# Row sums' accumulators and late results in PSUM, new load sizes and a burst of unread products in a cross-entropy kernel

## The chip, the cores and the metric

One core of a Trainium2 chip runs the program. ScalarE, VectorE and TensorE are its engines here; they run side by side and wait for one another, and for transfers (DMA), by counters called semaphores. SBUF and PSUM are its two on-chip memories. The metric is the device time of one execution in microseconds (us). A kernel's time is the median of its runs; most kernels here spread by 0.2 to 0.7 us from run to run, so a difference of a few tenths needs several runs of both kernels on the same chip. "Same" means within 2% with the whole of the 95% interval.

## The reference

For each of 256 rows of 32000 fp32 logits, the result is the negative logarithm of the softmax at the row's label.

```python
log_probs = logits - np.max(logits, axis=-1, keepdims=True)
log_probs = log_probs - np.log(np.sum(np.exp(log_probs), axis=-1, keepdims=True))
return np.array([-log_probs[i, labels[i]] for i in range(batch)])
```

The kernel computes it as log(sum of exp(x)) minus the label's logit, without the maximum, as log(sum × exp(-x_label)). The logits are drawn from a normal distribution, so no exp overflows.

## The kernel before

Two rows lie behind one another on each of 128 partitions: 64000 columns in 14 loads, counted from 0. ScalarE takes each load's exp in place, and its accumulator gives the sum of that load. Every exp is therefore two instructions on the engine: the exp itself and a read that puts the accumulator into a column of `parts`. Load 3 holds the end of row 0 and the start of row 1 and takes two exps. One VectorE reduction per row adds its columns, one TensorE product per row multiplies the sum with exp(-x_label) (on a diagonal) and brings all partitions into one lane, and ScalarE takes the logarithm of that. The last load's sum skips the reduction and is added by a second product for row 1.

```python
CHUNKS = [
    1024, 14528, 13376, 8960, 7168, 5056, 3584,
    2816, 2176, 1536, 1280, 1024, 768, 704,
]
# ...
parts = [small.tile([P, n_of[r]], F32, name=f"parts{r}") for r in range(ROWS)]   # SBUF
s_last = small.tile([P, 1], F32, name="s_last")
lane = [psum.tile([1, P], F32, name=f"lane{r}") for r in range(ROWS)]
# ...
def exps(i):
    t, base = tiles[i]
    for a, b, r in pieces[i]:
        if i == last:
            acc = s_last[:, :]
        else:
            acc = parts[r][:, seen[r]:seen[r] + 1]
            seen[r] += 1
        nc.scalar.activation(
            out=t[:, a - base:b - base], in_=t[:, a - base:b - base],
            func=AF.Exp, accum_out=acc,
        )
# ... the end:
for i in range(done, last):
    exps(i)
    if i == turn:                      # the load in which row 0 ends
        nc.vector.reduce_sum(out=sums[:, 0:1], in_=parts[0][:, :], axis=mybir.AxisListType.X)
        nc.tensor.matmul(lane[0][:, :], sums[:, 0:1], diag[0][:, :], start=True, stop=True)
    if i == turn + 1:
        log_row(0)
nc.vector.reduce_sum(out=sums[:, 1:2], in_=parts[1][:, :], axis=mybir.AxisListType.X)
nc.tensor.matmul(lane[1][:, :], sums[:, 1:2], diag[1][:, :], start=True, stop=False)
exps(last)
nc.tensor.matmul(lane[1][:, :], s_last[:, :], diag[1][:, :], start=False, stop=True)
log_row(1)
# ... store
```

## Time and profile before

| | before |
|---|---|
| time, median of 3 (range) | 84.87 us (84.86 to 84.89) |
| span of the profile | 83.0 us |
| ScalarE busy | 58.2 us, 70% |
| DMA queue of the logits, share of 16 engines | 93.0% |
| last exp starts | 79.17 us |
| logarithm of row 1 starts | 80.71 us |

The prediction shows the lines on which it rests. Two more of the timeline of before are needed here, around the exp of load 4 (columns: start, length in us, engine, line, operation, result and source, shapes):

```profile
56.08 0.19 ACT L120 ACTIVATION_READ_ACCUMULATOR x<-x 128x1 f32 x1
56.17 6.16 ACT L120 ACTIVATE x<-x 128x7168 f32<-128x7168 f32 x1
```

The next exp starts 0.09 us after the accumulator read starts, while the read's record (0.19) is still open. This distance, read start to next exp start, is called the step below.

### The profile page before, as it was taken

Reading aid. Unit: us, or ns where it says so; the run is one execution under the profiler, and the core shown is the slowest. Engines: PE = TensorE matmul, PEld = TensorE weight load, DVE = VectorE, ACT = ScalarE, POOL = GpSimd, SP = SyncE. Lnnn points to the kernel's source line nnn. Section 1 sums busy time; section 2 is a strip of 40 time slices with the busy share of each in tenths; the row PEclk is TensorE's granted clock in tenths of the full one; section 3 lists DMA queues with packets and bytes.
Section 4 is the critical chain, followed back from the end, with each engine's and each line's share of the span. In section 5 each row is a group of like instructions: output and inputs, shape, how many; then the busy total and the mean of one; then the engine's idle time right before and its main releaser. Section 6 shows DMA issues by size and latency. Waiting matters only on the chain.

```text
span 83.0 us, 126 instructions
## 1 busy us (share of the span) xinstructions
PE 1.7 (2%) x6; PEld 0.3 (0%) x6; DVE 0.8 (1%) x4; ACT 58.2 (70%) x34; POOL 3.0 (4%) x10
## 2 busy tenths in 40 slices
PE   0000000000000000000000002000000000000050
PEld 0000000000000000000000000000000000000000
DVE  0000000000000000000000020000000000000000
ACT  6230000000899999029999999999999999999960
POOL 3000000000640000000000000000000000000000
DMA  4999999999999999979989799999999999999600
GB/s 87 614 448 448 448 448 448 448 448 413 412 412 413 412 413 412 412 328 501 449 380 535 307 401 428 442 451 390 458 411 414 431 434 408 400 415 405 262 0 0
DMA packets 2226, 32.77 MB, mean 395 GB/s; under 512 B 433, under 2 KB 434, under 8 KB 1202
## 3 DMA queue, kind: packets, MB, share of 16 engines
q1 hardware_dynamic: 2018, 32.77, 93.0%
q10 hardware_dynamic: 144, 0.00, 0.1%
q0 software_dynamic: 64, 0.00, 0.1%
HBM read 32.77 MB, written 0.00 MB: 395 GB/s over the span
## 4 chain that ended last, share of the span: by engine, by line
DMA 43%; ACT 37%; issue 14%; PE 1%; SPq 0%; DVE 0%
DMA x<-in_logits_dram 43%; ACT x L120 26%; ACT x_tail L120 11%; PE lane L172 1%; PE lane L170 1%; ACT res L128 1%; SPq L108 0%; DVE sums L169 0%; ACT eg L159 0%
## 5 line engine op out<-in xcount | busy, mean ns | idle before, releaser
L120 ACT ACTIVATE x<-x 128x1024 f32<-128x1024 f32 (+7 forms) x8 | 46.3, 5786 | 21.3 <-DMA x<-in_logits_dram 21.3
L120 ACT ACTIVATE x_tail<-x_tail 128x2816 f32<-128x2816 f32 (+6 forms) x7 | 9.9, 1412 | 0.0
L144 POOL DMA_INDIRECT g<-in_logits_dram,idx x2 | 2.1, 1037 | 0.6 <-issue 0.3
L99 ACT ACT_TABLE_LOAD x1 | 1.3, 1283 | 0.8 <-PEq L191 0.8
L166 PE MATMUL lane<-diag,sums 128*1 128x128 f32 x2 | 0.6, 397 | 51.4 <-DVE sums L165 51.4
L120 ACT ACTIVATION_READ_ACCUMULATOR x<-x 128x1 f32 x8 | 1.5, 186 | 0.0
L120 ACT ACTIVATION_READ_ACCUMULATOR x_tail<-x_tail 128x1 f32 x7 | 1.3, 185 | 0.0
L170 PE MATMUL lane<-diag,sums 128*1 128x128 f32 x2 | 0.6, 397 | 27.5 <-DVE sums L169 27.5
L128 ACT ACTIVATE res<-lane 1x128 f32<-1x128 f32 x2 | 0.5, 266 | 0.7 <-PE lane L172 0.7
L161 DVE TENSOR_SCALAR diag<-ident,eg 128x128 f32<-128x128 f32 x2 | 0.5, 285 | 48.5 <-ACT eg L159 48.5
L142 POOL TENSOR_TENSOR idx<-idx,lbl 128x2 int32<-128x2 int32 x1 | 0.2, 193 | 19.6 <-DMA lbl<-in_labels_dram 19.6
L172 PE MATMUL lane<-diag,s_last 128*1 128x128 f32 x2 | 0.6, 398 | 0.0
L169 DVE TENSOR_REDUCE sums<-parts 128x1 f32<-128x10 f32 x1 | 0.2, 164 | 27.9 <-ACT x_tail L120 27.9
masks.py:199 POOL TENSOR_SCALAR_AFFINE_SELECT ident<-ident 128x128 f32<-128x128 f32 x1 | 0.3, 292 | 0.1
L166 PEld LDWEIGHTS lane<-diag,sums 128*1 128x1 f32 x2 | 0.1, 80 | 51.4 <-DVE sums L165 51.4
masks.py:197 POOL MEMSET ident<- 128x128 f32 x1 | 0.2, 194 | 0.0
L159 ACT ACTIVATE eg<-g 128x2 f32<-128x2 f32 x1 | 0.2, 187 | 0.0
L165 DVE TENSOR_REDUCE sums<-parts 128x1 f32<-128x4 f32 x1 | 0.2, 157 | 2.2 <-ACT x L120 2.2
L170 PEld LDWEIGHTS lane<-diag,sums 128*1 128x1 f32 x2 | 0.1, 80 | 28.0 <-DVE sums L169 28.0
L140 POOL IOTA idx<- 128x2 int32 x1 | 0.1, 120 | 0.5 <-POOLq L191 0.5
L191 POOL MEMSET const-uint8-127<- 128x1 uint8 x1 | 0.1, 118 | 0.0
L191 POOL MEMSET const-bfloat16-1.0<- 128x1 bf16 x1 | 0.1, 112 | 0.0
(3 smaller groups left out, 0.3 us busy)
## 6 DMA issues: line engine op xcount, KB each, us to landing
x<-in_logits_dram SPq DMA_DIRECT2D x1, 7264.0 KB, 20.1
x<-in_logits_dram SPq DMA_DIRECT2D x1, 6688.0 KB, 35.7
x<-in_logits_dram SPq DMA_DIRECT2D x1, 4480.0 KB, 45.8
x<-in_logits_dram SPq DMA_DIRECT2D x1, 3584.0 KB, 53.9
x<-in_logits_dram SPq DMA_DIRECT2D x1, 2528.0 KB, 59.3
x<-in_logits_dram SPq DMA_DIRECT2D x1, 1792.0 KB
x_tail<-in_logits_dram SPq DMA_DIRECT2D x1, 1408.0 KB, 21.0
x_tail<-in_logits_dram SPq DMA_DIRECT2D x1, 1088.0 KB, 23.1
```

The lines of the kernel that those rows point to most:

```text
L99: nc.scalar.preload_act_table_set("natural_log_exp_and_others")
L120: nc.scalar.activation(out=t[:, a - base:b - base], in_=t[:, a - base:b - base], func=AF.Exp, accum_out=acc,)
L128: nc.scalar.activation(out=res[0:1, r:ROWS * P:ROWS], in_=lane[r][:, :], func=AF.Ln)
L142: nc.gpsimd.tensor_add(out=idx[:, :], in0=idx[:, :], in1=lbl[:, 0:2 * ROWS:2])
L144: nc.gpsimd.indirect_dma_start(out=g[:, r:r + 1], out_offset=None, in_=logits[:, :], in_offset=bass.IndirectOffsetOnAxis(ap=idx[:, r:r + 1 ...
L159: nc.scalar.activation(out=eg[:, :], in_=g[:, :], func=AF.Exp, scale=-1.0)
L161: nc.vector.tensor_scalar_mul(diag[r][:, :], ident[:, :], eg[:, r:r + 1])
L165: nc.vector.reduce_sum(out=sums[:, 0:1], in_=parts[0][:, :], axis=mybir.AxisListType.X)
L166: nc.tensor.matmul(lane[0][:, :], sums[:, 0:1], diag[0][:, :], start=True, stop=True)
L169: nc.vector.reduce_sum(out=sums[:, 1:2], in_=parts[1][:, :], axis=mybir.AxisListType.X)
L170: nc.tensor.matmul(lane[1][:, :], sums[:, 1:2], diag[1][:, :], start=True, stop=False)
L172: nc.tensor.matmul(lane[1][:, :], s_last[:, :], diag[1][:, :], start=False, stop=True)
```

## The change

Its intent is to shorten the small costs of the end: accumulator reads and exp results go to PSUM, the load sizes are fitted to the cost per exp that this should give, and a burst of products whose results nobody reads keeps TensorE busy so that the last real product runs at its higher clock. The core of the diff:

```diff
 CHUNKS = [
-    1024, 14528, 13376, 8960, 7168, 5056, 3584,
-    2816, 2176, 1536, 1280, 1024, 768, 704,
+    1024, 15808, 12832, 9248, 6816, 4992, 3648,
+    2688, 2016, 1504, 1152, 928, 736, 608,
 ]
+WARM_FROM = 8
+WARM = 12
+TO_PSUM = 9
...
-    parts = [small.tile([P, n_of[r]], F32, name=f"parts{r}") for r in range(ROWS)]
+    acc_tile = psum.tile([P, sum(n_of)], F32, name="parts")
+    parts = [acc_tile[:, :n_of[0]], acc_tile[:, n_of[0]:]]
+    out_tile = psum.tile([P, max(CHUNKS[TO_PSUM:])], F32, name="x_out")
...
-    lane = [psum.tile([1, P], F32, name=f"lane{r}") for r in range(ROWS)]
+    lane_tile = psum.tile([1, ROWS * P], F32, name="lane")
+    lane = [lane_tile[:, r * P:(r + 1) * P] for r in range(ROWS)]
+    warm = psum.tile([1, P], F32, name="warm")
...
-                out=t[:, a - base:b - base],
+                out=t[:, a - base:b - base] if i < TO_PSUM else out_tile[:, :b - a],
...
+            if i == WARM_FROM:
+                at = starts[i] - tiles[i][1]
+                col = tiles[i][0][:, at:at + 1]
+                for _ in range(WARM):
+                    nc.tensor.matmul(warm[:, :], col, diag[0][:, :], start=True, stop=True)
```

More of the change, by code (lines that the diff above doesn't have):

```diff
@@ L128, in log_row @@
         nc.scalar.activation(
-            out=res[0:1, r:ROWS * P:ROWS], in_=lane[r][:, :], func=AF.Ln
+            out=res[0:1, r:ROWS * P:ROWS], in_=lane[r], func=AF.Ln
         )
@@ L164 @@
             if i == turn:
-                nc.vector.reduce_sum(out=sums[:, 0:1], in_=parts[0][:, :], axis=mybir.AxisListType.X)
-                nc.tensor.matmul(lane[0][:, :], sums[:, 0:1], diag[0][:, :], start=True, stop=True)
+                nc.vector.reduce_sum(out=sums[:, 0:1], in_=parts[0], axis=mybir.AxisListType.X)
+                nc.tensor.matmul(lane[0], sums[:, 0:1], diag[0][:, :], start=True, stop=True)
             if i == turn + 1:
                 log_row(0)
-        nc.vector.reduce_sum(out=sums[:, 1:2], in_=parts[1][:, :], axis=mybir.AxisListType.X)
-        nc.tensor.matmul(lane[1][:, :], sums[:, 1:2], diag[1][:, :], start=True, stop=False)
+            if i == WARM_FROM:
[3 more added lines that the diff above has]
+                    nc.tensor.matmul(warm[:, :], col, diag[0][:, :], start=True, stop=True)
+        nc.vector.reduce_sum(out=sums[:, 1:2], in_=parts[1], axis=mybir.AxisListType.X)
+        nc.tensor.matmul(lane[1], sums[:, 1:2], diag[1][:, :], start=True, stop=False)
         exps(last)
-        nc.tensor.matmul(lane[1][:, :], s_last[:, :], diag[1][:, :], start=False, stop=True)
+        nc.tensor.matmul(lane[1], s_last[:, :], diag[1][:, :], start=False, stop=True)
         log_row(1)
```

## The prediction

> **What bounds the kernel now.** I read the page's slices first, then the chain that ended last, then the timeline of the last 20 us, then the transfers. Two rows of the slices (40 slices of 2.08 us, busy tenths), ScalarE and the DMA engines:
>
> ```profile
> ACT  6230000000899999029999999999999999999960
> ...
> DMA  4999999999999999979989799999999999999600
> ```
>
> DMA is full from the first slice to 78 us. ScalarE waits for the first two large loads and is full from 37 us on. So two things run side by side for the last 40 us, and whichever is later at the last load sets the end. The chain gives the last steps (start, length in us):
>
> ```profile
> 66.80 3.36 ACT x L120 x3
> 70.15 9.12 ACT x_tail L120 x12
> 79.27 0.02 issue
> 79.30 0.17 DVE sums L169
> 79.47 0.04 issue
> 79.51 0.59 PE lane L170 x2
> 80.10 0.59 PE lane L172 x2
> 80.69 0.02 issue
> 80.71 0.27 ACT res L128
> ```
>
> The chain goes through ScalarE without a wait, then two 0.59 us TensorE products, the logarithm and the store. The timeline shows the steps of ScalarE:
>
> ```profile
> 62.04 0.33 SPq L108 DMA_DIRECT2D x_tail<-in_logits_dram  x1
> 62.24 0.19 ACT L120 ACTIVATION_READ_ACCUMULATOR x<-x 128x1 f32 x1
> 62.33 0.26 ACT L128 ACTIVATE res<-lane 1x128 f32<-1x128 f32 x1
> 62.49 4.40 ACT L120 ACTIVATE x<-x 128x5056 f32<-128x5056 f32 x1
> ...
> 72.50 0.18 ACT L120 ACTIVATION_READ_ACCUMULATOR x_tail<-x_tail 128x1 f32 x1
> 72.59 2.00 ACT L120 ACTIVATE x_tail<-x_tail 128x2176 f32<-128x2176 f32 x1
> 74.50 0.19 ACT L120 ACTIVATION_READ_ACCUMULATOR x_tail<-x_tail 128x1 f32 x1
> ...
> 79.17 0.77 ACT L120 ACTIVATE x_tail<-x_tail 128x704 f32<-128x704 f32 x1
> ```
>
> An exp of 2176 columns starts at 72.59, its accumulator read at 74.50: 1.91 us, which is 2176/1.2 = 1.813 plus 0.093. The next exp starts 0.093 after that read. So an exp costs its columns/1.2 plus 0.187 us, and each instruction starts 93 ns before the one ahead of it has ended. The last load is issued at 62.04:
>
> ```profile
> x_tail<-in_logits_dram SPq DMA_DIRECT2D x1, 352.0 KB, 16.9
> ```
>
> It lands at 62.04 + 16.9 = 78.95, and its exp starts at 79.17. **ScalarE is only 0.22 us behind DMA.** No reordering of ScalarE's work can gain more than that before the last exp; the rest must come after it.
>
> **What the skill says.** "Perfetto Trace Analysis", section Optimizing Scalar/DVE Operations: a ScalarE operation has about 93 ns of access on SBUF and 51 on PSUM, a VectorE one 60 and 125, and the profiled latency is about twice this because the acknowledgement overlaps with the next instruction. The trace agrees on SBUF: 93 ns and records of 186. It agrees on a PSUM source: the logarithm of 128 elements starts at 62.33 and the next exp 0.156 us later, 0.107 + 0.049. No run shows a PSUM destination yet. "ScalarE: Activation LUTs", section What ACT_TABLE_LOAD costs, gives 186 ns + 0.833 N and an overlap of 93, as the trace does. "PSUM — Partial Sum Buffer", section PSUM bank collisions raise a hardware error, says two engines may not touch one bank at once; that is why putting both rows' accumulators into one PSUM tile must bring waits. "TensorE: Matmul & The Clock Gate", section Part 1: The HAM clock gate, says the array runs at half clock until a free-running window of about 3.4 us has been busy, and falls back after an idle one. The trace has no clock record; its product takes 0.60 us from weights to semaphore, which I fit as two passes (the page counts two matmuls a product) of 0.213, 256 cycles at the page's 1.2 GHz, plus 0.17.
>
> **The change, part by part.**
>
> *Sizes.* From the transfer records a row of 58112 bytes takes 2.154 us on one engine and one of 2816 bytes 0.115, so a column costs 1.18 ns and a load about 0.09 us more. There are still 14 loads of the same total, so the last load lands at 78.95 as before. The loads before it move: load 2 (now 15808 + 12832 columns in) lands 736 columns, 0.87 us, later, at 37.74. Behind it ScalarE has 12832 and all later columns. With the old 0.187 per exp I step through, each start the later of landing and previous exp: load 3 at 48.73, load 4 at 56.81, 62.84, 67.19, 70.42, 72.84, 74.71, 76.15, 77.30, 78.26, and the last at 79.06. That is 0.11 before today's 79.17. The last exp is 96 columns shorter, another 0.08. Sum -0.19.
>
> *PSUM accumulators.* The built program of the changed kernel shows what the diff hides. In the kernel before, no exp behind another waits for it (one has a wait long satisfied). In the changed one **almost every exp waits on ScalarE's own semaphore**, for the accumulator read just before it, since they write one PSUM tile. So the 93 ns overlap is lost: the next exp starts not 93 ns after the read starts but after the read has ended, plus the semaphore. The semaphore shows 9 ns after a read's end, and a waiting engine starts about 22 ns later (VectorE at 79.296 after the update at 79.273). A read into PSUM I estimate at 2 x 51 = 102 ns from the skill's figures, so the step is 102 + 31 = 133 ns in place of 93: +0.04 per exp. It is paid by the second part of load 3 and by every load from 6 to 13: nine times, +0.36. Loads 3 and 5 hide it under the small exp and the logarithm.
>
> *The wait on VectorE.* The exp of load 4 now waits for the first row's sum, which itself waits for both parts of load 3. The path is: read 0.102, semaphore 0.032, reduction 0.16, semaphore and start 0.035, so 0.33 in place of 0.093: +0.24. ScalarE is on the path here and no slack takes it back, because all later landings are at its heels, not ahead.
>
> *Results in PSUM.* The next instruction starts after the source's access, which stays SBUF, so I give this nothing for the pace. The last accumulator stays in SBUF.
>
> *Unread products.* Twelve at 2 x 0.213 = 0.43 us make 5.1 us at the low clock. They start when the exp of load 8 is done, at about 75, and end about 79 to 80. If the clock rises, the last product takes 0.60 - 0.21 = 0.39 us: -0.21. The row-1 product is due about 0.24 us into the last exp, at 79.9, so the twelve are just out of the way.
>
> *Sum.* -0.11 - 0.08 - 0.21 + 0.36 + 0.24 = +0.20 us: 84.87 + 0.20 = **85.07**, say 85.0 with some weight on the rivals below.
>
> **Rivals.**
>
> *The new waits cost nothing* and a read into PSUM lets the next exp go after the skill's 51 ns. Then an exp costs about 0.15 (0.093 + 0.051) in place of 0.187, and ScalarE meets every landing within 0.1 us. For it: the new sizes fit exactly such an overhead; someone who saw exps fall behind would have put more columns in front. Against it: in this trace consumers of ScalarE's semaphore start only after the read's end. The last exp would start at 78.97: 79.17 to 78.97 is -0.20, with -0.08 and -0.21 about 84.4.
>
> *The waits cost more.* A read into PSUM may record 140 ns, between my 102 and the 186 that it has on SBUF: nine more of 0.038 and one on the VectorE path make +0.38, so about 85.4.
>
> *TensorE's clock does not rise, or the burst ends late.* Weight columns are one wide, and the window runs freely, so it may not count as busy in time. Without a rise +0.21; and with all twelve at the low clock from 75.2 they end at 80.3, after row 1's product is due, and would push it and the last product by up to 0.5. For it: 5.1 us is not much more than 3.4. About 85.3 to 85.6.
>
> *DMA becomes the bound.* It nearly is: nothing can start the last exp before 78.97. It caps the gain; it does not add.
>
> **Range and chances.** I give the costly self-waits about two chances in three, spread from 84.9 to 85.4 by the length of the read, and free ones one in three, near 84.4. The clock shifts either by 0.2. The middle of it all is 85.0; a range of 84.3 to 85.6 holds both. A change of 2% is 1.7 us. The gains stop at about 0.5 us since DMA bounds them, and the losses I can count stop near 1.0, so nearly all the chance is on within 2%.
>
> **What would show it.** In the changed profile: the start of the last exp (79.6 if the waits cost what I say, 79.0 if nothing); the time from an accumulator read's start to the next exp's (133 ns, against 93 before and about 51 for the rival) and the record of a read into PSUM (102); a gap of about 0.33 us ahead of the 6816-column exp; the last landing (78.95 unless the transfers change); the last product from its start to the logarithm's start (0.39 warm, 0.60 cold), and when the twelve end against row 1's product. The prediction is wrong in size if the read's record is not near 102, and wrong in kind if the read-to-exp step is shorter than 93 in spite of the waits, or if the late end comes from TensorE.

## More of the kernel before

The profile's span ends with the last instruction that it records. The profiled run took 84.82 us, so 1.79 us of its time lies outside its span (83.03 us in the trace).

## The result, and the profile after

| | before | after |
|---|---|---|
| time, median (range), 4 runs each | 84.88 us (84.86 to 84.90) | 86.37 us (86.19 to 86.52) |
| profiled run: time, span | 84.82, 83.0 us | 86.45, 84.3 us |
| exp of load 2 starts | 36.90 us | 38.28 us |
| last exp starts | 79.17 us | 80.73 us |
| logarithm of row 1 starts | 80.71 us | 82.00 us |

The ratio of after to before is 1.0174, with a 95% interval of 1.0152 to 1.0196: "same" by the 2% rule, but clearly longer, and outside the predicted range of 84.3 to 85.6. A ratio here is always the mean time of one kernel's fast runs over that of the other's of the same rounds, so it is not quite the ratio of the medians.

The slices of after, for TensorE, ScalarE and the DMA engines (40 slices of 2.11 us, busy tenths):

```profile
PE   0000000000000000000000000002000000009950
...
ACT  6220000000099999928999999998999999999970
...
DMA  4999998699989999979898999999999999999100
```

The first 8 in ScalarE's row behind its wait for load 2 is the slice in which that load's exp starts (38.28), and the other 8, at 57 to 59 us, is where ScalarE waits for VectorE. In TensorE's row the burst is seen near the end. DMA ends as before, near 79 us. Its slices of 8 and 6 early on are not idle time: the packet records, summed over windows of 2 us, cover 98 to 100% of the 16 engines there. Packets of load 1 last 2.33 us, longer than a slice, and every kernel with the new first sizes shows such a dip in this row.

The groups of accumulator reads, before and then after (busy us, mean ns of one):

```profile
L120 ACT ACTIVATION_READ_ACCUMULATOR x<-x 128x1 f32 x8 | 1.5, 186 | 0.0
```

```profile
L129 ACT ACTIVATION_READ_ACCUMULATOR x<-x 128x1 f32 x8 | 1.2, 152 | 0.0
L129 ACT ACTIVATION_READ_ACCUMULATOR x_out<-x_tail 128x1 f32 x5 | 0.7, 139 | 0.0
```

The reads did get shorter: 186 ns into SBUF, 152 into PSUM. In the second group one is the last, which still goes to SBUF and takes 186; the other four take 128 each. But shorter reads did not make shorter steps, as the timeline of after shows:

```profile
57.38 0.15 ACT L129 ACTIVATION_READ_ACCUMULATOR x<-x 128x1 f32 x1
57.56 0.16 DVE L174 TENSOR_REDUCE sums<-parts 128x1 f32<-128x4 f32 x1 [7.64 <-ACT x L129]
57.76 5.88 ACT L129 ACTIVATE x<-x 128x6816 f32<-128x6816 f32 x1 [0.23 <-DVE sums L174]
...
73.90 0.15 ACT L129 ACTIVATION_READ_ACCUMULATOR x_tail<-x_tail 128x1 f32 x1
74.08 1.88 ACT L129 ACTIVATE x_tail<-x_tail 128x2016 f32<-128x2016 f32 x1
...
76.08 4.39 PE L182 MATMUL warm<-diag,x_tail 128*1 128x128 f32 x24 [17.71 <-ACT x_tail L129]
77.42 0.13 ACT L129 ACTIVATION_READ_ACCUMULATOR x_out<-x_tail 128x1 f32 x1
77.58 1.13 ACT L129 ACTIVATE x_out<-x_tail 128x1152 f32<-128x1152 f32 x1
...
80.73 0.68 ACT L129 ACTIVATE x_out<-x_tail 128x608 f32<-128x608 f32 x1
80.74 0.17 DVE L183 TENSOR_REDUCE sums<-parts 128x1 f32<-128x10 f32 x1 [23.01 <-ACT x_out L129]
80.96 0.38 PE L184 MATMUL lane<-diag,sums 128*1 128x128 f32 x2 [0.48 <-DVE sums L183]
81.59 0.38 PE L186 MATMUL lane<-diag,s_last 128*1 128x128 f32 x2 [0.25 <-ACT x_out L129]
82.00 0.27 ACT L137 ACTIVATE res<-lane 1x128 f32<-1x128 f32 x1 [0.47 <-PE lane L186]
```

Three things are to be seen. From 57.38 to 57.76 the exp of load 4 waits for a reduction on VectorE that needs the read before it; in before there were 0.09 us at this place. At 73.90 and 77.42 the next exp starts after the read has *ended* (0.18 and 0.16 after the read's start), not inside it. And the last product takes 0.38 in place of the 0.59 of before: the burst did what it is for.

The chain of waits of after shows the same from its side (start, length in us): the read now stands whole on the path, with a gap behind it.

```profile
73.90 0.16 ACT x_tail L129
74.06 0.02 issue
74.08 0.92 ACT x_tail L129
```

Finally the transfers that land late. The issues of loads 1 and 2 in after (size, us from issue to landing):

```profile
x<-in_logits_dram SPq DMA_DIRECT2D x1, 7904.0 KB, 22.1
x<-in_logits_dram SPq DMA_DIRECT2D x1, 6416.0 KB, 37.0
```

Load 2 has its semaphore at 38.20 us, 0.46 later than the 37.74 of the prediction, and its exp starts at 38.28, 0.52 later than the 37.76 that follow from it with the 22 ns of before. ScalarE stood idle until then. The other 0.06 are a cost of the change: an instruction of these programs carries one wait. In before the exp itself waits for its load and starts 22 ns after the semaphore. In after it waits for ScalarE's own semaphore, the wait for the load is an instruction of its own ahead of it, and it starts 82 ns after. In all twenty profiles the exps of loads 1 and 2 start 22 to 23 ns behind their landing, or 82 to 88 where the wait stands apart.

### The profile page after: what moved, and what is told of

It is laid out like the page before. It is cut to its first block, busy times and chain, and to the rows that moved or that the text cites. A ratio compares the mean times of both kernels' runs of the same rounds, so it can differ in the third digit from the quotient of the medians.

```text
span 84.3 us, 186 instructions
## 1 busy us (share of the span) xinstructions
PE 5.7 (7%) x30; PEld 2.8 (3%) x30; DVE 0.8 (1%) x4; ACT 58.8 (70%) x34; POOL 3.0 (4%) x10
## 4 chain that ended last, share of the span: by engine, by line
DMA 44%; ACT 30%; issue 22%; PE 0%; SPq 0%; DVE 0%; ACTq 0%
DMA x<-in_logits_dram 44%; ACT x L129 24%; ACT x_tail L129 3%; ACT x_out L129 2%; ACT res L137 1%; PE lane L186 0%; SPq L117 0%; DVE sums L174 0%; ACTq L129 0%
## 5 line engine op out<-in xcount | busy, mean ns | idle before, releaser
L129 ACT ACTIVATE x<-x 128x1024 f32<-128x1024 f32 (+7 forms) x8 | 46.9, 5863 | 21.9 <-DMA x<-in_logits_dram 21.6
L182 PE MATMUL warm<-diag,x_tail 128*1 128x128 f32 x24 | 4.4, 365 | 17.7 <-ACT x_tail L129 17.7
L129 ACT ACTIVATE x_out<-x_tail 128x1504 f32<-128x1504 f32 (+4 forms) x5 | 5.0, 995 | 0.2
L129 ACT ACTIVATE x_tail<-x_tail 128x2688 f32<-128x2688 f32 (+1 forms) x2 | 4.3, 2162 | 0.1
L182 PEld LDWEIGHTS warm<-diag,x_tail 128*1 128x1 f32 x24 | 2.6, 110 | 19.8 <-ACT x_tail L129 18.2
L129 ACT ACTIVATION_READ_ACCUMULATOR x_out<-x_tail 128x1 f32 x5 | 0.7, 139 | 0.0
L129 ACT ACTIVATION_READ_ACCUMULATOR x_tail<-x_tail 128x1 f32 x2 | 0.3, 154 | 0.0
```

Of the source, the lines that this page charges most:

```text
L129: nc.scalar.activation(out=t[:, a - base:b - base] if i < TO_PSUM else out_tile[:, :b - a], in_=t[:, a - base:b - base], func=AF.Exp, accu ...
L182: nc.tensor.matmul(warm[:, :], col, diag[0][:, :], start=True, stop=True)
```

## The experiments

**The theory** after this comparison: the time is lost because the accumulators of both rows lie in one PSUM tile, so each exp waits for the end of the read just before it, and once for VectorE; the wait is longer than predicted. **The rivals:** a read into PSUM is slow by itself, wait or no wait; results in PSUM slow the exps; the burst on TensorE is in the way; or the new sizes are at fault. Eighteen experiments ran, in pairs and groups on the same chips (x1 is the changed kernel itself and x2 is e4 once more). All gave correct results. By the 2% rule each is "same" against before but for x2, whose interval crosses 2% and is "unclear"; the rounds resolve less than that.

### One part alone, on top of before (e1, e2, e3)

e1 takes the list of new sizes alone. e2 takes the accumulators alone, with the old sizes:

```diff
-    parts = [small.tile([P, n_of[r]], F32, name=f"parts{r}") for r in range(ROWS)]
+    acc_tile = psum.tile([P, sum(n_of)], F32, name="parts")
+    parts = [acc_tile[:, :n_of[0]], acc_tile[:, n_of[0]:]]
```

e3 takes the twelve products alone (`warm`, `WARM_FROM = 8`, `WARM = 12`, as in the change). Before in the same rounds: 84.91 us.

> The kernel before with the new sizes alone, accumulators and results in SBUF. If the sizes are worth what the prediction gave them (last exp 0.11 earlier and 0.08 shorter) it takes 84.7 us and load 2 lands at 37.7. If the late landing of load 2 in the changed kernel (38.2) comes from the sizes (rows of 63232 bytes) it takes about 85.1, with load 2 at 38.2. ScalarE's step per exp stays 0.187 in both.

> The kernel before with the accumulators in PSUM alone, old sizes. If the new self-waits are the main cost, the step from an accumulator read to the next exp is 185 ns in place of 93 for eight exps (+0.74), the exp of load 4 waits 0.38 for VectorE in place of 0.09 (+0.29), sum about +1.0: 85.9 us. If the cost of the change lies mostly in the transfers or the sizes, this one is at most +0.4: 85.3.

> The kernel before with the twelve unread products alone. If they raise TensorE's clock in time and are out of the way by 79.5, the last product takes 0.39 in place of 0.60: 84.67 us. If the clock rises at a time of its own, some executions gain nothing or wait for the products: between 84.6 and 85.2, with a spread of some 0.3 us over the runs.

| kernel | median, us (range, runs) | ratio to before (95%) |
|---|---|---|
| e1, sizes | 84.72 (84.57 to 85.02, 6) | 0.9967 (0.9942 to 0.9991) |
| e2, accumulators | 86.23 (86.19 to 86.89, 6) | 1.0166 (1.0132 to 1.0199) |
| e3, products | 84.64 (84.52 to 84.87, 6) | 0.9960 (0.9933 to 0.9987) |

The accumulators alone cost 1.32 us; sizes and products gain 0.19 and 0.27. e2 came 0.3 over the 85.9 expected; in its profile 0.16 of that lies outside the span, and as much comes from exps that start out of a wait, both below. The timeline of e2, at the old sizes, has one step with a wait and one without:

```profile
73.22 0.15 ACT L121 ACTIVATION_READ_ACCUMULATOR x_tail<-x_tail 128x1 f32 x1
73.40 2.02 ACT L121 ACTIVATE x_tail<-x_tail 128x2176 f32<-128x2176 f32 x1
...
80.34 0.15 ACT L121 ACTIVATION_READ_ACCUMULATOR x_tail<-x_tail 128x1 f32 x1
80.39 0.78 ACT L121 ACTIVATE x_tail<-x_tail 128x704 f32<-128x704 f32 x1
```

The first step is 0.18, as in after (the wait on VectorE is there too, 0.38 ahead of the exp of load 4). The second tells the rivals apart: the last exp writes its accumulator to SBUF and waits for no read, and it starts 0.05 us after a read into PSUM has started. So **a read into PSUM is not slow**; without a wait its step is 51 ns, shorter than the 93 of SBUF. The wait is what costs. The burst and the sizes are out as causes.

### The wait taken away by other tiles (e5), and the results alone (e8, e6)

Accumulators stay in PSUM, but those of a row alternate between two tiles, so an exp depends on the read two before it, which has long ended. The reductions and products double (two per row). Results are back in SBUF:

```diff
-    acc_tile = psum.tile([P, sum(n_of)], F32, name="parts")
-    parts = [acc_tile[:, :n_of[0]], acc_tile[:, n_of[0]:]]
+    half = [[(n_of[r] + 1 - k) // 2 for k in range(2)] for r in range(ROWS)]
+    parts = [[psum.tile([P, half[r][k]], F32, name=f"parts{r}{k}") for k in range(2)] for r in range(ROWS)]
...
-                acc = parts[r][:, seen[r]:seen[r] + 1]
+                acc = parts[r][seen[r] % 2][:, seen[r] // 2:seen[r] // 2 + 1]
...
+        for k in range(2):
+            nc.vector.reduce_sum(out=sums[:, 2 + k:3 + k], in_=parts[1][k][:, :], axis=mybir.AxisListType.X)
+            nc.tensor.matmul(lane[1], sums[:, 2 + k:3 + k], diag[1][:, :], start=k == 0, stop=False)
```

e8 is the changed kernel with only the results back in SBUF (`TO_PSUM = 14`). e6 is the changed kernel with the accumulators back in SBUF (`parts` as before) and the results of the last five in PSUM.

> The changed kernel with results in SBUF and the accumulators spread over four PSUM tiles, each row's taking two in turn, so that an exp waits for the accumulator read two before its own, which is long done, and the exp of load 4 does not wait for VectorE. If the self-waits and that wait are the cost, the step from an accumulator read to the next exp falls from 185 to about 51 ns, the last exp starts about 79.2 in place of 80.7, and it takes 84.4 to 84.9 us. If the accumulators in PSUM cost time by themselves, it stays above 85.5.

> The changed kernel with all results in SBUF, accumulators in one PSUM tile. If a result in PSUM only shortens the accumulator read's record (153 to 128 ns) three steps get 0.026 longer, and the last exp no longer waits for the read before it (0.16 to 0.05): together -0.03, 86.3 us, as the changed kernel. If results in PSUM are a main cost: below 86.0; if they help: above 86.6.

> The changed kernel with the accumulators back in SBUF; the results of the last five exps still go to one PSUM tile, so the last four exps still wait for the exp before. Expected if each self-wait costs what it seems: the wait on VectorE and the waits of loads 3 and 6 to 9 are gone, four steps are 0.19 in place of 0.093: 85.5 us. If results in PSUM cost nothing: 84.5, as the sizes with the products should.

| kernel (same chip; before 84.88) | median, us (range, runs) | ratio (95%) |
|---|---|---|
| e8, one tile, results in SBUF | 85.90 (85.85 to 86.16, 5) | 1.0114 (1.0087 to 1.0142) |
| e5, two tiles a row, results in SBUF | 84.47 (84.22 to 85.63, 6) | 0.9952 (0.9914 to 0.9991) |
| e6, accumulators in SBUF, results in PSUM | 85.04 (84.86 to 85.28, 6) | 1.0015 (0.9988 to 1.0042) |

e8 and e5 have the same sizes, burst and place of results. They differ in the tiles of the accumulators, and by 1.43 us. Some 0.2 of that lies outside the span (last experiments below); the rest shows the dependence on one tile as the main cause. In the built program each of these tiles starts in a PSUM bank of its own, so tile and bank aren't told apart here. Nor did any run leave the waits out with one tile, so whether the chip needs them stays open. With one SBUF tile a row (before) the program has none. The timeline of e5:

```profile
78.40 0.15 ACT L125 ACTIVATION_READ_ACCUMULATOR x_tail<-x_tail 128x1 f32 x1
78.45 0.81 ACT L125 ACTIVATE x_tail<-x_tail 128x736 f32<-128x736 f32 x1
...
80.20 1.06 PE L182 MATMUL lane<-diag,sums 128*1 128x128 f32 x4
81.05 0.42 PE L184 MATMUL lane<-diag,s_last 128*1 128x128 f32 x2
```

The step is 0.05, and up to 0.10 where the exp waited for its own load (that of load 7 starts 82 ns after its landing), where the changed kernel has 0.16 to 0.19. The profiled run was the slowest of its six (85.63, slow and left out of the ratio), and the last two lines show why: here TensorE's clock did not rise during the burst, the burst ran from 75.13 to 80.2, and it pushed row 1's products and the last one back. That is the prediction's third rival, in one run of a kernel whose other five took 84.22 to 85.18. e8's profile, a fast run, has it on a smaller scale: there too the clock did not rise during the burst, row 1's product starts at 80.77, 0.15 after its reduction ended, and the last one takes 0.59.

e6 shows results in PSUM by themselves. They make the last four exps wait for the read before them, since all write one result tile, at a step of 0.217 (186 ns of a read into SBUF plus 31): 76.06 to 76.27 for the first. The pace of an exp does not change: 1504 columns go from exp to read in 1.35 us with the result in PSUM (74.71 to 76.06) and also in SBUF (75.12 to 76.47 in e1). The time came 0.5 us under the 85.5 expected, which was more than its own terms (84.5 plus four times 0.1) give; in its profile load 2's exp starts at 37.76, exactly on time. e8 came 0.4 under its expectation of 86.3 too, with load 2 at 37.89.

### Parts taken together and apart (e4, e7, and x1 with x2)

e4 is the changed kernel without the twelve products. It was to show their gain against the changed kernel's first runs, which were not of the same rounds. x1 is the changed kernel unchanged and x2 is e4 again, both on one chip. e7 is before with sizes and products, without anything new in PSUM.

```diff
-            if i == WARM_FROM:
-                at = starts[i] - tiles[i][1]
-                col = tiles[i][0][:, at:at + 1]
-                for _ in range(WARM):
-                    nc.tensor.matmul(warm[:, :], col, diag[0][:, :], start=True, stop=True)
```

> The changed kernel without the twelve unread products. If they gain 0.21 there: 86.58 us, and if the spread of the changed kernel's runs (0.33) is TensorE's clock, the spread goes to 0.05. If the spread is the transfers', it stays at 0.3.

> The kernel before with the new sizes and the unread products, everything in SBUF. If the two gains add (sizes 0.19, products 0.27 measured alone): 84.45 us. If the sizes, which bring ScalarE close to the landings, leave no room: 84.7.

> The changed kernel again, for a comparison on one chip with the one without products. 86.2 to 86.5 us. In its profile the last product takes 0.39 us if TensorE's clock has risen by then, 0.60 if not.

> The changed kernel without the unread products, on the same chip. If the products gain what the last product's time says: 0.21 over the changed kernel. If their gain is lost in executions in which the clock rises late: the same as the changed kernel within 0.1, with less spread.

| kernel | median, us (range, runs) | ratio (95%) | exp of load 2 starts |
|---|---|---|---|
| e4, changed without products | 86.17 (86.08 to 86.37, 4) | 1.0137 (1.0104 to 1.0169) | 38.00 |
| x1, changed kernel again | 86.09 (85.97 to 86.19, 4) | 1.0143 (1.0127 to 1.0160) | 37.80 |
| x2, changed without products | 86.34 (86.09 to 87.09, 6) | 1.0186 (1.0154 to 1.0218) | 37.83 |
| e7, sizes and products | 84.81 (84.46 to 85.19, 6) | 0.9986 (0.9955 to 1.0018) | 38.40 |

e4 missed its expectation of 86.58: it came out 0.20 *under* the changed kernel's first median. On one chip the order is right: x2 is 0.25 over x1, which fits the 0.21 of the shorter last product (the two intervals just overlap). So the changed kernel's first four runs, at 86.37, were themselves some 0.3 us on the late side (x1 came 0.1 under its expected 86.2 to 86.5), and for the profiled runs x1 says of what: load 2's exp starts at 37.80 there, against 38.28. e7 is a miss of another kind: gains of 0.19 and 0.27 alone make 0.07 together, with load 2 0.64 us late in its profile.

**What is open about load 2.** With the old first sizes that exp starts between 36.84 and 37.05 in eight of ten profiles, and at 37.28 and 37.73 in two (f3, g2). With the new ones (15808 and 12832 columns) it starts within 0.13 us of the reckoned 37.76 in five of ten, and 0.24 to 0.64 late in the others. In the packet records of the late ones, from 1 to 13 of load 1's 128 packets take 2.4 to 3.2 us in place of 2.33. The records don't name the engine; if packets are joined end to start into 16 chains, a chain with such a packet stays behind from there (in e1, e5 and e7 one with 0.67 to 0.84 us too much lands last). Their number alone doesn't do it: e8 has 15 of up to 2.59 us and its exp is 0.13 late. DMA is busy throughout. That the larger load makes this likelier is suggested, not shown: it happens with the old sizes too (in g2 one packet takes 3.01 in place of 2.15), and before's own runs reach 85.44.

### The rest that the span does not hold (f1, f2, f3, g1, g2, g3)

The changed kernel's four runs are 2.09 to 2.18 us longer than their spans; before's are 1.75 to 1.84. These 0.34 us lie outside everything that the profile shows. Among the kernels the difference goes with the number of instructions in ScalarE's program, not with the time of the run. The instruction total of the profile shows that number: 186 in after against 126 is 48 of the burst (24 loads of weights and 24 passes) and 12 more on ScalarE, waits that take an instruction of their own. ScalarE's part of the built program, where an exp and its read count as one, is 23 in before, 35 in after. Rival: it comes from PSUM.

To separate the two, exps of one column, whose results nobody reads, were put behind the first exp, where ScalarE idles for 16 us. f1, f2, g2 and g3 are before with 12, 30, 11 and 13 of them, g1 is the changed kernel with 3, and f3 is e10 (below) with 6 (37 instructions, not the 38 of its expectation, since one wait falls away). All but g1 (four runs) have two runs each. For f1:

```diff
+    scr = small.tile([P, 12], F32, name="scr")
...
+        if i == 0:
+            for k in range(12):
+                nc.scalar.activation(out=scr[:, k:k + 1], in_=t[:, k:k + 1], func=AF.Exp)
```

> The kernel before with 12 one-column exps more on ScalarE, in its idle time behind the first load (35 instructions in the body, as many as the changed kernel). If the number of ScalarE instructions makes the time outside the span, measured time less span goes from 1.79 to about 2.1 and the time to 85.2; if not, 1.79 and 84.9.

> The same with 30 one-column exps (53 instructions). If the number counts: 2.1 or more outside the span; if not, 1.79.

> The kernel with alternating accumulators and no unread products, with 6 one-column exps (38 instructions in place of 32). If the number counts: outside the span 2.1 in place of 1.78; if not, 1.78.

> The changed kernel with three one-column exps behind the first load, 37 instructions in ScalarE's body. If the program's length is the cause: 1.79 outside the span in place of 2.12, and about 85.9 us. If the PSUM tile is the cause: 2.12 and 86.2 us.

> The kernel before with 11 one-column exps, 34 instructions. The kernels with one PSUM tile and 34 had 1.94 to 2.02 outside the span: if length alone counts, this one has that too.

> The kernel before with 13 one-column exps, 36 instructions. Between 35 (2.12) and 37 (1.79): either.

| instructions on ScalarE | kernels | time minus span, us | median, us |
|---|---|---|---|
| 23 | before, e1, e3, e7 | 1.75 to 1.85 | |
| 27 | e6 | 1.76 to 1.83 | |
| 32 | e5, e9, e10 | 1.75 to 1.85 | |
| 34 | e2, e8; g2 | 1.93 to 2.06; 1.98, 2.04 | g2 85.41 |
| 35 | after, x1, x2, e4; f1 | 2.08 to 2.19; 2.11, 2.17 | f1 85.14 |
| 36 | g3 | 1.93, 1.95 | g3 85.09 |
| 37 | g1; f3 | 1.77 to 1.84; 1.78, 1.85 | g1 85.77, f3 84.72 |
| 53 | f2 | 1.77, 1.81 | f2 84.94 |

Spans are on record to 0.1 us, so a difference in the table is good to 0.05. In the profiled runs, whose spans the traces hold to the nanosecond, the picture is sharper: 2.12 to 2.13 in all five with 35 instructions, 1.94 to 2.02 in the three with 34, 1.95 with 36, and 1.78 to 1.82 in the rest.

f1 is before with no more PSUM than before and has the changed kernel's 2.1; its span is 83.0 and its last exp starts at 79.13, as in before. g1 is the changed kernel with *more* work, and it loses the excess: 85.77 us (85.67 to 85.89, 4 runs), ratio 1.0107 (1.0090 to 1.0123), on a chip on which x1 had 86.09. So what counts is the length of ScalarE's program and not PSUM. f2's expectation, that more instructions cost more, failed: why 34 to 36 cost it, while fewer and more do not, stays open, since the trace doesn't cover it.

### A version that keeps what gains (e9, e10)

e9 is e5 with the old first sizes, three sizes of its own behind them, and 14 products that start one load earlier. e10 is e9 without products.

```diff
-    1024, 15808, 12832, 9248, 6816, 4992, 3648,
+    1024, 14528, 13376, 9632, 7040, 5120, 3648,
     2688, 2016, 1504, 1152, 928, 736, 608,
...
-WARM_FROM = 8
-WARM = 12
+WARM_FROM = 7
+WARM = 14
```

> Accumulators alternating in four PSUM tiles, results in SBUF, the first two large loads in the old sizes (14528, 13376) with the new tail behind them, and 14 unread products from load 7 on, about 2 us earlier. If the late landing of load 2 comes from the 15808-column load, it lands at 36.9 as before; ScalarE meets the last landing at 79.0, and with the clock up in every execution it takes 84.3 us with a spread under 0.3. If the engines' lateness is chance, the spread stays at 0.7, and if the clock is not up in every execution some runs are 0.3 to 1 us longer.

> The same without the products: 0.21 more than with them, 84.5 us, and a spread no smaller than the transfers' own.

| kernel (same chip as x1, x2; before 84.91) | median, us (range, runs) | ratio (95%) |
|---|---|---|
| e9 | 84.34 (84.12 to 84.81, 6) | 0.9938 (0.9915 to 0.9962) |
| e10 | 84.54 (84.44 to 84.91, 6) | 0.9966 (0.9947 to 0.9985) |

The timeline of e9, ScalarE's last steps and TensorE's last product:

```profile
72.95 0.14 ACT L125 ACTIVATION_READ_ACCUMULATOR x_tail<-x_tail 128x1 f32 x1
73.00 1.86 ACT L125 ACTIVATE x_tail<-x_tail 128x2016 f32<-128x2016 f32 x1
...
78.94 0.14 ACT L125 ACTIVATION_READ_ACCUMULATOR x_tail<-x_tail 128x1 f32 x1
78.99 0.69 ACT L125 ACTIVATE x_tail<-x_tail 128x608 f32<-128x608 f32 x1
...
79.83 0.38 PE L184 MATMUL lane<-diag,s_last 128*1 128x128 f32 x2
```

Every step is 50 to 52 ns. The last exp starts at 78.99, 0.18 before that of before and 1.74 before that of the changed kernel. e9 is the fastest kernel, 0.57 us under before and 1.75 under the changed one (86.09 on the same chip), yet still within 2% of before. Its last exp starts 0.15 after the last landing (78.84), so there is little more to gain ahead of it, as the prediction said of any version. Products gain 0.20 here (84.54 to 84.34). e9's runs spread by 0.69 us, not by the hoped-for 0.3; the profiled one says nothing of the longest.

## Why the prediction was wrong

The direction was the one that the sum gave (+0.20), and each part that it named was there. The size was not: +1.49 by the medians. The table goes through the sum, against the profiled runs of the changed kernel's first measurement (86.45) and of x1 (85.97), both compared with the profiled run of before (84.82).

| term of the sum | predicted | after | x1 |
|---|---|---|---|
| new sizes (kept as reckoned; e1 alone measured -0.19) | -0.19 | -0.19 | -0.19 |
| exp of load 2 starts later than reckoned | 0 | +0.52 | +0.04 |
| nine self-waits, step above 93 ns | +0.36 | +0.72 | +0.72 |
| wait on VectorE | +0.24 | +0.29 | +0.29 |
| exp that starts out of a wait | 0 | +0.17 | +0.16 |
| last product at the higher clock | -0.21 | -0.21 | -0.21 |
| outside the span | 0 | +0.34 | +0.34 |
| sum | +0.20 | +1.64 | +1.15 |
| measured | | +1.63 | +1.15 |

- **The mechanism was right.** The step "almost every exp waits on ScalarE's own semaphore" was read from the built program and held: nine steps without the overlap, one wait on VectorE. e2 shows both alone, and e5 against e8 shows that they go when the tile is split. One detail was misread: the last exp's accumulator is in SBUF, and its wait comes from the result tile that it shares with the exp before (in e8, with results in SBUF, its step is 0.05). And what the prediction cites on PSUM banks is about two engines; it bears on the wait on VectorE, not on ScalarE's waits for itself, which only the built program shows.
- **The step that failed** is "A read into PSUM I estimate at 2 x 51 = 102 ns from the skill's figures". The record is 153 ns behind an exp with its result in SBUF and 128 behind one with its result in PSUM. The second half of that step was right: 32 ns from the read's end to the exp. So a step is 0.185 or 0.160 (0.176 once), not 0.133. The nine sum to 1.554 us, of which 9 × 0.093 = 0.837 was there before: +0.72, twice the +0.36. On the path through VectorE the same error makes 0.38 in place of 0.33. The rival "the waits cost more" assumed 140 ns, nearer but still short.
- **Terms were missing.** An exp that starts out of a wait takes about 16 ns more to its accumulator read than one that starts inside the read before it: 2688 columns take 2.349 us (2.240 + 0.109), where columns/1.2 plus 0.093 would give 2.333. Ten or eleven times, that is the +0.17. The kernel before had it in view: its exp of 13376 columns, started out of a wait for DMA, took 11.256 to its read, also 0.109 over columns/1.2. And the wait for load 2 as an instruction of its own is 0.06 of the start of that exp in both columns; without it load 2 was 0.46 late in after and 0.03 early in x1.
- **The results in PSUM** were given nothing for the pace, and the pace is indeed unchanged (e6). They shortened three steps from 0.185 to 0.160 and made the last one 0.160 in place of the 0.05 of e8: together +0.03, which is already in the +0.72.
- **The sizes and the products** came as predicted when alone. The last landing came at 79.18 in place of 78.95 (78.69 in x1, where load 2 was on time), and it did not matter, since ScalarE was far behind it. The burst ended at 80.47 and row 1's product started at 80.96, so the burst was not in the way in after; in e5 it was, once.
- **The range was too narrow for another reason.** With the right size of the waits the sum would have been 85.07 + 0.36 + 0.05 = 85.5, still inside. The prediction lets the losses that it can count stop near 1.0, and +1.49 was measured. What carried it out of the range were the 16 ns, the 0.34 us outside the span, which no view of a trace shows, and in the first runs the late landing of load 2. In x1 that landing was on time and the kernel was still outside, at 86.09.

The clock forecast is a partial hit. By the trace's clock records, which the spacing of the burst's passes bears out (213 ns, then 109), the clock rose 3.3 us after the burst began in after, between 2.7 (e7) and 4.8 (e3) in other profiles, and in e8 and e5 only after 5.9 and 6.0, when the burst was over.

## What to carry to other kernels

Before putting small results into PSUM, look at what the tile makes dependent: the same 153 ns read costs a step of 51 ns where nothing waits for it and 185 where the next instruction does, and two tiles used in turn were worth more than everything else in this change. Where an instruction must wait for the one before, count the earlier one's *recorded* end, measured on the same kind of operation, plus the semaphore, plus the longer start of the one that waited. A wait too many on an instruction also costs where it pushes the wait for a load into an instruction of its own (0.06 us here). And compare the change of the measured time with the change of the profile's span; where they differ, part of the answer is not in the trace.

## What the Trainium skill lacked or had wrong

- "Perfetto Trace Analysis", section Optimizing Scalar/DVE Operations: its 51 ns on PSUM is right for the start of the next instruction behind an accumulator read (50 to 52 ns in e2, e8, e9 and e10). Its rule that the profiled latency is about twice that does not hold for this read: it records 128 to 177 ns (153 most often), where twice 51 is 102. It does hold on SBUF (186 for 93).
- The same section lacks what a wait on the instruction just ahead costs on ScalarE: 160 to 185 ns from read to exp with accumulators in PSUM and 217 in SBUF, against 51 and 93 without the wait, and 16 ns more in the exp that waited.
- "ScalarE: Activation LUTs", section Step-by-step: what each stage is for, calls PSUM the lower-latency destination. The runs agree for the record (an exp of 1504 columns is recorded as 1.40 us into PSUM and 1.44 into SBUF) but show no gain where instructions follow without a wait: 1.35 us from exp to read for both.
- "TensorE: Matmul & The Clock Gate", section Part 1: The HAM clock gate, puts the rise at about 3.4 us of activity in a free-running window. The runs bear out the window (in all nine profiles with a burst the clock then stays up for 3.413 or 6.827 us) but not 3.4 us as the delay: with fp32 products and one-column weights the rise came 2.7 to 6.0 us after the start, so a burst of 5.3 us is no sure thing.
- No page that was read tells why the time outside the span should go with the length of ScalarE's program: 1.8 us for most kernels, 1.93 to 2.19 when it has 34 to 36 instructions.
- No page that was read has the size of what held up load 1 and load 2 here: packets of 2.4 to 3.2 us in place of 2.33, and an exp of load 2 up to 0.64 us late. The cause stays open.
- No page that was read has what it costs on ScalarE when the wait for a landing is an instruction of its own: the exp starts 82 to 88 ns after the landing's semaphore, against 22 to 23 where it carries the wait itself.
